# A hybrid layer on one core: the sum projection contracts over all 16 row tiles in PSUM, residual rows move into the last projection, ya is split one tile a product

## The chip, the core and the metric

The kernel runs on one core of a Trainium2 chip. A core has TensorE (PE, with its weight loads as PEld), VectorE (DVE), ScalarE (ACT), GpSimd (POOL) and SyncE (SP), each with its own queue of instructions that it takes in order, and DMA engines that SP, ACT and POOL hand transfers to. SBUF is the working memory on the chip, PSUM the eight banks of 128 x 512 fp32 that TensorE writes its products into. The metric is the time of one launch on the device in microseconds (us); the median of three runs before was 1457.02 us (1455.95 to 1457.52).

## The reference

One layer over 1024 positions and 1024 channels, fp32, tolerances of fp32. Cut to what matters here:

```python
h = layer_norm(x, ln_in_g, ln_in_b)
proj = h @ w_in                                  # u, b_gate, c_gate, z_a, z_s, xbc, dt, g_a, g_s
y_a = silu(z_a) * b_gate * conv3(c_gate * u)
y_a = y_a @ w_a_out                              # 1024 -> 1024, the first projection
y_s = ssd_scan(...) + d_skip * xs                # 2048 channels in 4 groups
y_s = gated_group_rmsnorm(y_s, z_s, norm_s_g)
y_s = y_s @ w_s_out                              # 2048 -> 1024, the sum projection
mixed = sigmoid(g_a) * y_a + sigmoid(g_s) * y_s
out = mixed @ w_o                                # 1024 -> 1024, the last projection
h = layer_norm(2 ** 0.25 * h + out, ln_g, ln_b)
```

## The kernel before

**Precision.** Every operand of a product is split into a high part (rounded to fp32r) and the rest: ACT copies the high part, and `sub_split` (L106) subtracts it from the full value. A product is three matmuls for each 128 rows of contraction: high by high, high by rest, rest by high (`mm3`, L799 to L802). One such split of 128 x 512 elements costs one ACT copy and one subtraction.

**The stages.** The input projection is 44 pairs of output tiles; each pair is seven products of 12 matmuls (a Strassen-like scheme, products 1, 2, 6, 5, 7, 4, 3 in this order, 3 behind the next pair's 1). While it runs, the scan of the state space is woven in, and its gated rows go to DRAM (`gat_d`, and per group the reciprocal root `rst_d`). Then come 16 items of the first projection `("a", j, kh)`, 24 matmuls each, 32 items of the sum projection `("s", g, j)`, 24 matmuls each, and the last projection, 8 rows of 128 positions.

**The order.** The loop over `items` writes out the instructions of item n, then what earlier items left in `sums` and `later` for n. Weights are fetched five items ahead, their high part is copied three items ahead and the rest two items ahead, so that in VectorE's queue the weight split of item n+2 stands before the sums of item n. `pin` keeps the written order on every engine from item 21 to the end of the loop; behind it, in the last projection, a scheduler sets the order.

**From the input projection to the first.** `start_post` loads the eight tiles of y_a (`ya`). In products 2, 6, 5 and 7 of pair 43 `halves` splits two of them each: four ACT copies (L771) and four subtractions on VectorE, beside that product's own weight split and adds (L954, L980, L982) that free its PSUM banks.

**The sum projection.** It goes group by group, g = 0 to 3, and in each over the eight output tiles j. Each item contracts over the four row tiles of its group into two fresh banks (`p_ws`); `item_s` adds that to `acc[j]` in SBUF: a copy on ACT for g = 0 (L891), an add on VectorE after (L893), for g = 2 also times sg plus yg (L895, L896), for g = 3 the last product with sg, the sum and the split of the result m (L899, L900, L902). The y tiles for group g are loaded and split on the way (`prep_y`, L781 to L789), one tile every other item: a broadcast of `rst_d` (rb), the tile gt, one three-operand product on VectorE (L789), two copies on ACT, two subtractions on VectorE.

**The residual rows** alpha * h are made on the way in groups 1 and 2 (`residual`): load x, normalise on ACT (L862), times ag and plus ab on POOL (L863, L864, 128 x 1024 each), store to `res_d`; the last projection loads them again.

**The last projection** (`project`, `norm_out`): per row of positions 48 matmuls into two banks, VectorE adds the residual and takes statistics (L1073, L1074), a chain of small operations gives mean and scale (L89 to L103), ACT normalises (L1090), POOL multiplies by lg and adds lb (L1091, L1092), SP stores. The last row does most of its columns on VectorE (L1086, L1087).

Of the kernel before, what the change touches and what calls it, by code (L numbers as in the profile page):

```python
# [45 lines left out]
def trunk_kernel(ctx: ExitStack, tc: tile.TileContext, x, w_in, w_dt, w_a, w_s, w_o, par, con,  # L46
# [97 lines left out]
    def otile(name):  # L144
        return ap.tile([P, L], F32, tag="O", name=name, bufs=4)
# [59 lines left out]
    items += [("s", g, j) for g in range(G) for j in range(KT)]  # L205
# [575 lines left out]
    def prep_y(g, k):  # L781

        rb = otile(f"rb{g}_{k}")
        SP.dma_start(rb, rst_d[g].squeeze(0).partition_broadcast(P))
        y = otile(f"gt{4 * g + k}")
        SP.dma_start(y, gat_d[g][:, k, :])

        def work():
            V.scalar_tensor_tensor(y, y, pc(C_NG + 4 * g + k), rb, ALU.mult, ALU.mult)  # L789
            halves(f"y{g}", k, y, True)  # L790
        later.setdefault(now[0] + (2 if items[now[0]][0] == "s" else 1), []).append(work)
# [41 lines left out]

    def split_wo(k, hf_i, u):
        r = rawt(f"raw_wo{k}_{hf_i}")
        SP.dma_start(r, w_o[k, :, hcols[hf_i]])
        WO[k, hf_i] = u

        def work():
            S.activation(u[:, 0, :], r, AF.Copy)  # L840
            sub_split(u[:, 1, :], r, u[:, 0, :], V)
        if hf_i:
            work()
        else:
            later.setdefault(now[0] + 1, []).append(work)

    norm_t = {}

    def residual(s):

        if s == 0:
            for i, (n, src) in enumerate((("ag", ln_in_g), ("ab", ln_in_b))):
                t = norm_t[n] = full_unit(POST[20 + i], n)
                SP.dma_start(t, src.partition_broadcast(P))
# [3 lines left out]
        def work():
            if s == 0:
                for t in norm_t.values():  # L860
                    S.activation(t, t, AF.Copy, scale=ALPHA)
            S.activation(r, r, AF.Identity, bias=nb_t[:, s:s + 1], scale=rs_t[:, s:s + 1])  # L862
            Gp.tensor_tensor(r, r, norm_t["ag"], ALU.mult)  # L863
            Gp.tensor_tensor(r, r, norm_t["ab"], ALU.add)  # L864
            Gp.dma_start(res_d[s], r)
        later.setdefault(now[0] + 1, []).append(work)

    def item_s(g, j, hi, lo):
        if g == 0:
            acc[j] = xtile(j, f"acc{j}") if j < 7 else cv("acc7")  # L870
        ps = [pbank(f"p_ws{g}_{j}_{i}") for i in range(2)]
# [6 lines left out]
        if g in (1, 2) and j % 2 == 0:
            residual(4 * (g - 1) + j // 2)
        if g == 1 and j == KT - 1:  # L880
            load_gy(0)
        if g == 2 and j < KT - 1:
            load_gy(j + 1)
        if g == 2 and j == KT - 1 or g == 3 and j < KT - 1:
            load_gy((j + 1) % KT, ("sg",))
        def evac():
            for hf_i in range(2):
                sl = hcols[hf_i]
                part = acc[j][:, sl]
                if g == 0:  # L890
                    S.activation(part, ps[hf_i], AF.Copy)  # L891
                elif g < 3:
                    V.tensor_tensor(part, ps[hf_i], part, ALU.add)  # L893
# [282 lines left out]
```

## Time and profile before

| | |
|---|---|
| runs before, median (lowest to highest) | 1457.02 us (1455.95 to 1457.52) |
| the profiled execution | 1455.73 us |
| its span on the core | 1454.0 us |
| mean granted TensorE clock | 0.989 |
| input projection up to the first matmul of the first projection | 1061.5 us |
| first projection | 1061.5 to 1151.1 us |
| sum projection | 1151.1 to 1356.7 us |
| last projection up to its last matmul, and the tail | 1356.7 to 1445.6 us, to 1454.0 |

A row of the timeline is: start in us, length in us, engine, line, operation, output<-inputs with their shape, and in brackets how long the engine sat idle before it and what released it. A length includes time in which the instruction had started and was held. Row groups end in "busy us, mean ns | idle before them, and what ended it". A stage table has PE, PEld, DVE, ACT and POOL busy (with instruction counts), the granted clock (1.00 is full), the share of the DMA engines and GB/s.

### The profile page before, as it was taken

Reading aid. Unit: us, or ns where it says so; the run is one execution under the profiler, and the core shown is the slowest. Engines: PE = TensorE matmul, PEld = TensorE weight load, DVE = VectorE, ACT = ScalarE, POOL = GpSimd, SP = SyncE. Lnnn points to the kernel's source line nnn. Section 1 sums busy time; section 2 is a strip of 40 time slices with the busy share of each in tenths; the row PEclk is TensorE's granted clock in tenths of the full one; section 3 lists DMA queues with packets and bytes.
Section 4 is the critical chain, followed back from the end, with each engine's and each line's share of the span. In section 5 each row is a group of like instructions: output and inputs, shape, how many; then the busy total and the mean of one; then the engine's idle time right before and its main releaser. Section 6 shows DMA issues by size and latency. Waiting matters only on the chain.

```text
span 1454.0 us, 18639 instructions
## 1 busy us (share of the span) xinstructions
PE 1396.3 (96%) x6522; PEld 1102.6 (76%) x6522; DVE 1022.1 (70%) x1495; ACT 716.0 (49%) x1243; POOL 481.0 (33%) x374
## 2 busy tenths in 40 slices
PE   6999999999999999999999999999899999959997
PEld 4677878787777878777878878787678888847786
DVE  7957878877788787787887585776534338778763
ACT  3664556555665655575645656555621233112321
POOL 4012334535244444335453344444000004331054
PEclk9999999999999999999999999999999999989999
DMA  6022354454454454454734545544547736567331
GB/s 231 16 109 80 112 144 128 137 159 133 142 130 136 138 155 123 137 131 135 172 118 134 161 125 150 151 124 138 218 162 242 232 118 218 213 212 288 131 127 62
DMA packets 171901, 217.02 MB, mean 149 GB/s; under 512 B 11520, under 2 KB 116896, under 8 KB 171808
## 3 DMA queue, kind: packets, MB, share of 16 engines
q1 hardware_dynamic: 162128, 181.80, 42.2%
q10 hardware_dynamic: 8272, 29.81, 5.2%
q0 software_dynamic: 1408, 4.23, 0.7%
q8 instruction: 51, 0.84, 0.2%
q14 instruction: 42, 0.34, 0.1%
HBM read 160.97 MB, written 54.82 MB: 148 GB/s over the span
## 4 chain that ended last, share of the span: by engine, by line
PE 80%; DVE 10%; DMA 5%; ACT 3%; issue 2%; ACTq 0%; SPq 0%; POOL 0%; POOLq 0%; DVEq 0%
PE p L945 10%; PE p L947 10%; PE p L946 10%; PE pU L947 8%; PE pU L945 8%; PE pU L946 8%; DMA yg<-yag_d 3%; PE ya L659 2%; PE p_ws L800 2%; PE p_ws L802 2%; PE p_ws L801 2%; PE p_wa L802 2%; PE p_wa L801 2%; PE p_wa L800 2%; PE st L664 2%
## 5 line engine op out<-in xcount | busy, mean ns | idle before, releaser
L106 DVE TENSOR_TENSOR wlop<-raw_a,whip 128x512 fp32r<-128x512 f32 x210 | 180.8, 861 | 171.4 <-ACT whip L276 66.7
L945 PE MATMUL p<-b,whip 128*128 128x512 f32 x352 | 144.0, 410 | 4.3 <-DVE ob L954 4.3
L945 PE MATMUL pU<-t,whip 128*128 128x512 f32 x352 | 144.7, 412 | 3.0 <-ACT oa L980 3.0
L276 ACT ACTIVATE whip<-raw_a 128x512 fp32r<-128x512 f32 x210 | 127.6, 622 | 36.9 <-issue 10.5
L945 PE MATMUL p<-t,whip 128*128 128x512 f32 x352 | 141.8, 403 | 1.5 <-DVE oa L954 1.5
L947 PE MATMUL p<-t,wlop 128*128 128x512 f32 x352 | 139.2, 395 | 1.5 <-DVE wlop L106 1.5
L946 PE MATMUL p<-b,whip 128*128 128x512 f32 x352 | 139.9, 398 | 0.0
L947 PE MATMUL p<-b,wlop 128*128 128x512 f32 x352 | 139.7, 397 | 0.0
L947 PE MATMUL pU<-t,wlop 128*128 128x512 f32 x352 | 139.0, 396 | 0.5 <-DVE wlop L106 0.4
L946 PE MATMUL p<-t,whip 128*128 128x512 f32 x352 | 138.9, 395 | 0.0
L946 PE MATMUL pU<-t,whip 128*128 128x512 f32 x352 | 138.9, 395 | 0.0
L644 POOL TENSOR_TENSOR xw<-xd,dte_t 128x256 f32<-128x256 f32 x56 | 47.0, 840 | 259.0 <-DVE xd L630 259.0
L802 PE MATMUL p_ws<-y,wlos 128*128 128x512 f32 x256 | 104.3, 408 | 12.4 <-DVE wlos L106 12.4
L801 PE MATMUL p_ws<-y,whis 128*128 128x512 f32 x256 | 103.9, 406 | 5.2 <-DVE y L106 5.2
L800 PE MATMUL p_ws<-y,whis 128*128 128x512 f32 x256 | 103.6, 405 | 0.0
L236 POOL TENSOR_TENSOR s<-raw_a,raw_a 128x512 f32<-128x512 f32 x42 | 69.5, 1654 | 85.1 <-DVE wlop L106 74.0
L250 POOL TENSOR_TENSOR raw_a<-raw_a,s 128x512 f32<-128x512 f32 x42 | 66.0, 1572 | 95.4 <-issue 87.4
L863 POOL TENSOR_TENSOR rs<-rs,ag 128x1024 f32<-128x1024 f32 x8 | 19.5, 2444 | 231.4 <-ACT rs L862 231.4
L945 PEld LDWEIGHTS p<-b,whip 128*128 128x128 f32 x352 | 66.8, 190 | 27.4 <-issue 8.8
L106 DVE TENSOR_TENSOR wlop<-s,whip 128x512 fp32r<-128x512 f32 x84 | 80.1, 966 | 9.4 <-PE p L947 6.3
L610 ACT ACTIVATE em<-em,cum_t 128x128 f32<-128x128 f32 x256 | 81.3, 390 | 7.3 <-ACT ob L554 4.4
L945 PEld LDWEIGHTS pU<-t,whip 128*128 128x128 f32 x352 | 66.1, 188 | 20.0 <-ACT oa L980 4.3
(223 smaller groups left out, 3353.7 us busy)
## 6 DMA issues: line engine op xcount, KB each, us to landing
raw_a<-in_w_in_dram SPq DMA_DIRECT2D x168, 256.0 KB
em<-cum_d SPq DMA_DIRECT2D x64, 256.0 KB
xg_d<-cv ACTq DMA_DIRECT2D x16, 512.0 KB
xT<-xg_d SPq DMA_DIRECT2D x32, 256.0 KB
z<-zs_d SPq DMA_DIRECT2D x32, 256.0 KB
gat_d<-y SPq DMA_DIRECT2D x32, 256.0 KB
rb<-rst_d SPq DMA_DIRECT2D x16, 512.0 KB
gt<-gat_d SPq DMA_DIRECT2D x16, 512.0 KB
```

What stands on the lines that cost most here:

```text
L106: return eng.tensor_tensor(lo, full, hi.bitcast(F32), ALU.subtract)
L236: Gp.tensor_tensor(s1, r["a21"], r["a22"], ALU.add)
L250: Gp.tensor_tensor(a12, a12, s1s[p]["s2"], ALU.subtract)
L276: S.activation(flat(hi), src, AF.Copy)
L610: S.activation(em[:, h, :], em[:, h, :], AF.Relu, bias=cum_t[:, 8 * g + 4 * i + h, c:c + 1], scale=-1.0)
L644: Gp.tensor_tensor(xw, XD[n, i], dte_t[:, hs, c].unsqueeze(2).to_broadcast([P, HG, HD]), ALU.mult)
L800: PE.matmul(ps, lhsT=hi[:, k, :], rhs=u[:, 0, :], start=start, stop=False)
L801: PE.matmul(ps, lhsT=hi[:, k, :], rhs=u[:, 1, :], start=False, stop=False)
L802: PE.matmul(ps, lhsT=lo[:, k, :], rhs=u[:, 0, :], start=False, stop=stop)
L945: PE.matmul(ps, lhsT=hi[:, k, :], rhs=u[:, 0, :], start=first, stop=False, skip_group_check=True)
L946: PE.matmul(ps, lhsT=hi[:, k, :], rhs=u[:, 1, :], start=False, stop=False, skip_group_check=True)
L947: PE.matmul(ps, lhsT=lo[:, k, :], rhs=u[:, 0, :], start=False, stop=(k == 3), skip_group_check=True)
```

## The change

- The sum projection keeps its partial sums in PSUM. The items of j = 0 to 2 run as a wave: groups 0 and 1 for the three, then groups 2 and 3 for the three, with six banks open; from j = 3 on the four groups of one j follow each other. `acc` is gone; one evacuation for each j, after its last group, multiplies by sg and adds yg in place.
- All 16 y tiles are split before their group is due: tiles 0 to 7 during the first projection, 8 to 15 at its end and in the first items of the sum projection, by a table of places. They stay in SBUF until the end of the sum projection. rb is loaded once a group.
- m is split later: first halves of tiles 0 to 6 and the first halves of w_o in the last three items, the rest behind the last item, ahead of the last projection's first row on VectorE's queue.
- `residual` writes no DRAM. Rows 0 to 2 are made ahead of the last projection, row s+3 behind `norm_out(s)`.
- The last projection's order is pinned too.
- ya: `turn_ya` splits one tile in each of the products 2, 6, 5, 7, 4 and 3 of pair 43 and two in the first item of the first projection; the second half's subtraction goes to POOL.

```diff
-    items += [("s", g, j) for g in range(G) for j in range(KT)]
+    WAVE = 3
+    s_order = [(g, j) for gs in ((0, 1), (2, 3)) for j in range(WAVE) for g in gs]
+    s_order += [(g, j) for j in range(WAVE, KT) for g in range(G)]
+    items += [("s", g, j) for g, j in s_order]
...
+    def turn_ya(k):
+        halves("a", k, ya_raw[k], (2 * k, 2 * k + 1), eng=Gp)
...
         def rests():
-            for u, part in zip(us, parts):
-                sub_split(u[:, 1, :], part, u[:, 0, :], V)
+            for u, part, e in zip(us, parts, (V, eng or V)):
+                sub_split(u[:, 1, :], part, u[:, 0, :], e)
...
+        if k == 0:
+            rb_t[g] = cv(f"rb{g}")
+            SP.dma_start(rb_t[g], rst_d[g].squeeze(0).partition_broadcast(P))
...
+    a0, s0 = item_at["a", 0, 0], item_at["s", 0, 0]
+    y_at = {}
+    for t, i in enumerate((1, 3, 5, 6, 8, 10, 11, 13, 14, 15, 16, 17, 18, 19, 19, 20)):
+        y_at.setdefault(a0 + i, []).append(t)
...
     def residual(s):
-        r = full_unit(POST[22 + s % 2], f"rs{s}")
-        SP.dma_start(r, x[s * P:(s + 1) * P, :])
...
-            Gp.dma_start(res_d[s], r)
+        r = res[s]
+        S.activation(r, r, AF.Identity, bias=nb_t[:, s:s + 1], scale=rs_t[:, s:s + 1])
+        Gp.tensor_tensor(r, r, norm_t["ag"], ALU.mult)
+        Gp.tensor_tensor(r, r, norm_t["ab"], ALU.add)
...
-                mm3(ps[hf_i], hi, lo, k, Y[f"y{g}", k, hf_i], k == 0, k == 3)
+                mm3(ps[hf_i], hi, lo, k, Y["y", 4 * g + k, hf_i], g == 0 and k == 0, g == G - 1 and k == 3)
...
-                if g == 0:
-                    S.activation(part, ps[hf_i], AF.Copy)
-                elif g < 3:
-                    V.tensor_tensor(part, ps[hf_i], part, ALU.add)
...
+                V.tensor_tensor(M[j][:, sl], ps[hf_i], M[j][:, sl], ALU.mult)
+                V.tensor_tensor(M[j][:, sl], M[j][:, sl], gy[j][:, sl], ALU.add)
+                if j == KT - 1:
+                    split_m(j, hf_i, post_unit(31 if hf_i == 0 else 15, f"m{j}_{hf_i}"))
...
+    def split_m(j, hf_i, u):
+        part = M[j][:, hcols[hf_i]]
+        M[j, hf_i] = u
+        S.activation(u[:, 0, :], part, AF.Copy)
+        sub_split(u[:, 1, :], part, u[:, 0, :], V)
...
+    for n in norm_t.values():
+        S.activation(n, n, AF.Copy, scale=ALPHA)
+    residual(0)
+    for k in range(4, KT):
+        split_wo(k, 1, post_unit(4 + k, f"wo{k}_1"))
+    residual(1)
+    load_res(2)
+    for k, i in enumerate((12, 13, 14, 33, 34, 32)):
+        split_m(k, 1, post_unit(i, f"m{k}_1"))
+    split_m(6, 1, ap.tile([P, 2, HALF], F32R, tag="cv", name="m6_1", bufs=2))
+    load_norm("lg", ("c", 0), ln_g)
+    load_norm("lb", ("o", 2), ln_b)
+    residual(2)
...
-            if i == NP - 1 and j in (2, 6, 5, 7):
+            if i == NP - 1 and j in (2, 6, 5, 7, 4, 3):
...
-                for k in range(2):
-                    kk = 2 * (2, 6, 5, 7).index(j) + k
-                    halves("a", kk, ya_raw[kk])
+                turn_ya((2, 6, 5, 7, 4, 3).index(j))
...
         norm_out(s, 3 if s == NCH - 1 else 2)
+        if s + 3 < NCH:
+            residual(s + 3)
+        pin(True)
```

**VectorE, from pair 43 into the first projection.** Names: a_k0 and a_k1 are the halves of tile k of ya, wlop43_j the rest of the weights of product j of pair 43, wloa the same for the first projection, ob43 an output tile of pair 43 whose adds free the bank that the pair's last product needs. Before:

```order
L106 TENSOR_TENSOR a_41_9534<-ya4_9439,a_41_9534 128x512
L106 TENSOR_TENSOR a_50_9539<-ya5_9441,a_50_9539 128x512
L106 TENSOR_TENSOR a_51_9540<-ya5_9441,a_51_9540 128x512
L106 TENSOR_TENSOR wlop43_3_9549<-raw43_a12_9242,whip43_3_9516 128x512
L106 TENSOR_TENSOR a_60_9565<-ya6_9443,a_60_9565 128x512
L106 TENSOR_TENSOR a_61_9566<-ya6_9443,a_61_9566 128x512
L106 TENSOR_TENSOR a_70_9571<-ya7_9445,a_70_9571 128x512
L106 TENSOR_TENSOR a_71_9572<-ya7_9445,a_71_9572 128x512
L106 TENSOR_TENSOR wloa0_0_9581<-raw_a0_0_9480,whia0_0_9547 128x512
L954 TENSOR_TENSOR ob43_9551<-p4_43_9520,ob43_9551 128x512
```

Now, from the same place (its lines are those of the changed file):

```order
L106 TENSOR_TENSOR a_10_9488<-ya1_9425,a_10_9488 128x512
L106 TENSOR_TENSOR wlop43_4_9498<-raw43_a22_9238,whip43_4_9468 128x512
L106 TENSOR_TENSOR a_20_9513<-ya2_9427,a_20_9513 128x512
L106 TENSOR_TENSOR wlop43_3_9523<-raw43_a12_9234,whip43_3_9496 128x512
L106 TENSOR_TENSOR a_30_9539<-ya3_9429,a_30_9539 128x512
L106 TENSOR_TENSOR wloa0_0_9549<-raw_a0_0_9466,whia0_0_9521 128x512
L988 TENSOR_TENSOR ob43_9525<-p4_43_9500,ob43_9525 128x512
```

Ahead of that add of ob43 stand four subtractions of ya (a_00, a_10, a_20, a_30) where sixteen stood; the second halves are on POOL's queue.

**VectorE, behind the last evacuation of the sum projection.** wo_k_1 is the second half of tile k of w_o, m_k_1 the second half of tile k of the mixed rows, res0 the first residual row. Now:

```order
L106 TENSOR_TENSOR wo4_1_11429<-raw_wo4_1_11396,wo4_1_11429 128x512
L106 TENSOR_TENSOR wo5_1_11432<-raw_wo5_1_11398,wo5_1_11432 128x512
L106 TENSOR_TENSOR wo6_1_11435<-raw_wo6_1_11400,wo6_1_11435 128x512
L106 TENSOR_TENSOR wo7_1_11438<-raw_wo7_1_11402,wo7_1_11438 128x512
L106 TENSOR_TENSOR m0_1_11446<-sg0_10476,m0_1_11446 128x512
L106 TENSOR_TENSOR m1_1_11449<-sg1_10551,m1_1_11449 128x512
...
L106 TENSOR_TENSOR m6_1_11464<-sg6_11109,m6_1_11464 128x512
L1119 TENSOR_TENSOR res0_11408<-p_wo0_0_11476,res0_11408 128x512
```

All splits of m's second halves stand before the first row's evacuation; before, the splits of m came with the evacuations of group 3.

**POOL, in the last projection.** res_s is residual row s; ag, ab belong to the residual, lg, lb to the output. Before:

```order
L1091 TENSOR_TENSOR res0_11691<-res0_11691,lg_11551 128x1024
L1092 TENSOR_TENSOR res0_11691<-res0_11691,lb_11553 128x1024
L1091 TENSOR_TENSOR res1_11693<-res1_11693,lg_11551 128x1024
L1092 TENSOR_TENSOR res1_11693<-res1_11693,lb_11553 128x1024
L1091 TENSOR_TENSOR res2_11695<-res2_11695,lg_11551 128x1024
L1092 TENSOR_TENSOR res2_11695<-res2_11695,lb_11553 128x1024
```

Now:

```order
L1137 TENSOR_TENSOR res0_11408<-res0_11408,lg_11467 128x1024
L1138 TENSOR_TENSOR res0_11408<-res0_11408,lb_11469 128x1024
L904 TENSOR_TENSOR res3_11584<-res3_11584,ag_11404 128x1024
L905 TENSOR_TENSOR res3_11584<-res3_11584,ab_11406 128x1024
L1137 TENSOR_TENSOR res1_11410<-res1_11410,lg_11467 128x1024
L1138 TENSOR_TENSOR res1_11410<-res1_11410,lb_11469 128x1024
```

Between two normalised rows POOL now makes one residual row, three rows ahead; ahead of these rows it makes residual rows 0 to 2.

More of the change, by code (lines that the diff above doesn't have):

```diff
@@ L142, in full_unit, with otile @@
         return hp.tile([P, L], F32, tag=f"q{i}", name=name)
-    def otile(name):
-        return ap.tile([P, L], F32, tag="O", name=name, bufs=4)
+    n_o = [0]
+    def otile(name, i=None):
+        if i is None:
+            i = n_o[0] % 4
+            n_o[0] += 1
+        return ap.tile([P, L], F32, tag=f"O{i}", name=name)
     def cv(name):
@@ L779, in halves, with place, prep_y @@
             rests()
[L781 to L785, printed above, removed]
+    YP = list(range(16, 32)) + list(range(16))
+    GT = [("x", 4), ("x", 5), ("x", 6), ("o", 2), ("o", 3)]
+    rb_t = {}
+    def place(where, name):
+        kind, i = where
+        return xtile(i, name) if kind == "x" else otile(name, i) if kind == "o" else cv(name)
+    def prep_y(t):
+        g, k = divmod(t, 4)
+        if k == 0:
+            rb_t[g] = cv(f"rb{g}")
+            SP.dma_start(rb_t[g], rst_d[g].squeeze(0).partition_broadcast(P))
+        rb = rb_t[g]
+        y = place(GT[t % 5], f"gt{t}")
         SP.dma_start(y, gat_d[g][:, k, :])
         def work():
-            V.scalar_tensor_tensor(y, y, pc(C_NG + 4 * g + k), rb, ALU.mult, ALU.mult)
-            halves(f"y{g}", k, y, True)
-        later.setdefault(now[0] + (2 if items[now[0]][0] == "s" else 1), []).append(work)
+            V.scalar_tensor_tensor(y, y, pc(C_NG + t), rb, ALU.mult, ALU.mult)
+            halves("y", t, y, YP[2 * t:2 * t + 2], True)
+        later.setdefault(now[0] + 1, []).append(work)
     n_bank = [0]
@@ L847, in trunk_kernel, with load_gy @@
-    norm_t = {}
-    def residual(s):
[L851 to L854, printed above, removed]
-        r = full_unit(POST[22 + s % 2], f"rs{s}")
-        SP.dma_start(r, x[s * P:(s + 1) * P, :])
[L858 to L864, printed above, removed]
-            Gp.dma_start(res_d[s], r)
-        later.setdefault(now[0] + 1, []).append(work)
+    def load_gy(j):
+        M[j] = place(SG[j], f"sg{j}")
+        SP.dma_start(M[j], sgs_d[j])
+        gy[j] = otile(f"yg{j}", j % 2 if j < KT - 1 else 0)
+        SP.dma_start(gy[j], yag_d[j])
@@ L868, in item_s @@
     def item_s(g, j, hi, lo):
         if g == 0:
-            acc[j] = xtile(j, f"acc{j}") if j < 7 else cv("acc7")
-        ps = [pbank(f"p_ws{g}_{j}_{i}") for i in range(2)]
+            sy[j] = [pbank(f"p_ws{j}_{i}") for i in range(2)]
+        ps = sy[j]
         for hf_i in range(2):
             for k in range(4):
-                mm3(ps[hf_i], hi, lo, k, Y[f"y{g}", k, hf_i], k == 0, k == 3)
-        if g < 3 and j in (1, 3, 5, 7)[:4 if g < 2 else 2]:
-            y_next = 4 * g + 6 + j // 2
-            prep_y(y_next // 4, y_next % 4)
@@ L878, in item_s @@
[L878 to L885, printed above, removed]
+                mm3(ps[hf_i], hi, lo, k, Y["y", 4 * g + k, hf_i], g == 0 and k == 0, g == G - 1 and k == 3)
         def evac():
@@ L1027, in trunk_kernel @@
             item_a(i, j, hi, lo)
+            if i == 0 and j == 0:
+                turn_ya(6)
+                turn_ya(7)
         else:
             item_s(i, j, hi, lo)
+        for t in y_at.get(n, ()):
+            prep_y(t)
+        if n in gy_at:
+            load_gy(gy_at[n])
         if n == START - 1:
@@ L1093, in norm_out @@
         SP.dma_start(out[s * P:(s + 1) * P, sl], r[:, sl])
-    for s in range(3):
-        load_res(s)
     for s in range(NCH):
```

114 lines of the change are left out of this document (59 added, 55 removed).

## The prediction

> **What bounds the kernel now.** First the page's busy shares and the chain that ended last.
>
> ```profile
> PE 1396.3 (96%) x6522; PEld 1102.6 (76%) x6522; DVE 1022.1 (70%) x1495; ACT 716.0 (49%) x1243; POOL 481.0 (33%) x374
> PE 80%; DVE 10%; DMA 5%; ACT 3%; issue 2%; ACTq 0%; SPq 0%; POOL 0%; POOLq 0%; DVEq 0%
> ```
>
> TensorE carries four fifths of the chain, so the question is where it is not at its pace. Next, busy time by stage: the first projection (p_wa), the sum projection (p_ws) and the last one (p_wo), from first matmul to first matmul. The columns are PE, PEld, DVE, ACT and POOL busy with instruction counts, then granted clock, DMA share and GB/s.
>
> ```profile
> 1061.50:1151.10 89.60, 89.60 (x385) 71.81 (x385) 34.87 (x49) 19.05 (x30) 0.00 (x0) 1.00 0.64 214
> 1151.10:1356.70 205.60, 187.94 (x769) 148.20 (x769) 137.29 (x166) 60.17 (x98) 46.07 (x24) 0.96 0.60 206
> 1356.70:1445.60 88.90, 88.61 (x409) 73.03 (x407) 51.00 (x100) 17.84 (x26) 33.60 (x14) 1.00 0.28 107
> ```
>
> The first projection issues 384 matmuls in 89.6 us without a gap: 0.2333 us each, at clock 1.00. The sum projection has twice as many, 768, of the same shape, and would take 179.2 us. It takes 205.6: **26.4 us lost**, at clock 0.96. What PE waited for there, with total, times and longest, and its rows behind two kinds of waits:
>
> ```profile
> PE p_ws L802 <- DVE wlos L106: 12.4, 6, 3.6
> PE p_ws L801 <- DVE y L106: 5.2, 1, 5.2
> 1278.55 0.51 PE L802 MATMUL p_ws<-y,wlos 128*128 128x512 f32 x1 [3.58 <-DVE wlos L106]
> ...
> 1279.68 0.63 PE L802 MATMUL p_ws<-y,wlos 128*128 128x512 f32 x1
> 1280.11 0.63 PE L800 MATMUL p_ws<-y,whis 128*128 128x512 f32 x1
> ...
> 1288.61 0.50 PE L802 MATMUL p_ws<-y,wlos 128*128 128x512 f32 x1 [2.63 <-DVE wlos L106]
> ...
> 1344.23 0.50 PE L802 MATMUL p_ws<-y,wlos 128*128 128x512 f32 x1 [1.39 <-DVE wlos L106]
> ```
>
> The waits are 17.6 us, all for VectorE. The other 8.8 are their sequel: behind a long wait matmuls stand 0.43 us apart (1279.68 to 1280.11) instead of 0.23. So VectorE bounds this stage. Why it is late is in the rows of POOL and DVE side by side:
>
> ```profile
> 1196.81 1.28 DVE L106 TENSOR_TENSOR y<-gt,y 128x512 fp32r<-128x512 f32 x2
> 1209.18 2.40 POOL L863 TENSOR_TENSOR rs<-rs,ag 128x1024 f32<-128x1024 f32 x1 [167.70 <-ACT rs L862]
> 1211.65 2.72 POOL L864 TENSOR_TENSOR rs<-rs,ab 128x1024 f32<-128x1024 f32 x1
> 1209.21 5.72 DVE L106 TENSOR_TENSOR y<-gt,y 128x512 fp32r<-128x512 f32 x2
> L893 DVE TENSOR_TENSOR acc<-p_ws,acc 128x512 f32<-128x512 f32 x32 | 21.1, 679 | 0.0
> ```
>
> Two subtractions of y take 1.28 us alone, and 5.72 beside two POOL operations: each ends only behind the POOL operation that it met. I call this **the lock**; one VectorE operation with two SBUF inputs gets through per POOL operation. Operations that read PSUM are not held: L893 means 679 ns over the same stretch.
>
> **Part 1, the sum projection.** The change removes its 16 ACT and 32 DVE partial sums, moves all of y's splits ahead of their use, and moves the residual's POOL work out of the stage. Per four items of 5.6 us VectorE keeps four weight splits and one evacuation of four operations: 8 x 0.68 = 5.5 us of 22.4, with POOL idle. Each y tile costs about 2.6 us of DVE (1.28 for L789, 1.28 for its two subtractions), beside gates (L821) and weight splits (the last row):
>
> ```profile
> L789 DVE SCALAR_TENSOR_TENSOR gt<-gt,par_t,rb 128x1024 f32<-128x1024 f32 x16 | 20.4, 1278 | 8.8 <-DMA gt<-gat_d 8.8
> L821 DVE TENSOR_TENSOR sga<-p_wa,sga 128x512 f32<-128x512 f32 x16 | 10.2, 681 | 0.0
> L106 DVE TENSOR_TENSOR wlos<-raw_s,whis 128x512 fp32r<-128x512 f32 x32 | 22.0, 687 | 49.9 <-issue 28.5 <-PE p_ws L802 9.8 <-PE p_wa L802 6.9
> ```
>
> Sixteen tiles over the 22 items from a1 on are 42 us, beside 10.2 of gates and 15 of weight splits: 67 of 123 us. The order puts the last y work one item ahead of (3,0), which needs it, and a weight split two items ahead of its matmuls, so an 11 us delay is hidden. SP's queue also carries less: rb is loaded 4 times instead of 16. With 16 gt, 8 sga and 8 yag of 0.5 MB and 22 weights of 0.26 that is about 25 MB in 123 us, 200 GB/s, where the first projection moved 214 without holding PE. Here sga of row j+2 waits on SP for the store of row j, and gt and raw stand behind it; the store goes out 2 us after its gate, so SP is some 11 us ahead of need. I take **-26.4**, from -26.4 to -18 if half of the waits find another cause.
>
> **Part 2, ya.** From pair 43 into the first projection, PE stops four times:
>
> ```profile
> PE p L945 <- DVE oa L954: 1.5, 1, 1.5
> PE pU L945 <- ACT oa L980: 1.6, 1, 1.6
> PE p L947 <- DVE wlop L106: 1.5, 1, 1.5
> 1057.13 0.77 PE L945 MATMUL p<-b,whip 128*128 128x512 f32 x1 [4.11 <-DVE ob L954]
> 1061.55 0.39 PE L800 MATMUL p_wa<-a,whia 128*128 128x512 f32 x1
> 1049.22 2.17 ACT L771 ACTIVATE a<-ya 128x512 fp32r<-128x512 f32 x4
> 1053.29 2.49 DVE L106 TENSOR_TENSOR a<-ya,a 128x512 fp32r<-128x512 f32 x4
> 1056.30 0.68 DVE L954 TENSOR_TENSOR ob<-p,ob 128x512 f32<-128x512 f32 x1
> 1040.18 1.29 POOL L250 TENSOR_TENSOR raw_a<-raw_a,s 128x512 f32<-128x512 f32 x1
> ```
>
> A product is 12 matmuls, 2.8 us; two tiles in it cost ACT 2.17 and DVE 2.49 us beside their other work. With one tile ACT pays 1.1, DVE 0.6 and POOL 1.3 (L250 has its shape). The first stop is older and stays. The second loses the 1.1 us of ACT. The fourth, which starts the slow clock, hangs on the first add to ob43: ACT's copy of pU at about 1049.7 (after the copies of three tiles instead of six), then DVE's row order a_30, wloa0_0, ob43. Without the lock that add ends at 1052.1 and the first projection starts at 1054.9: 6.6 earlier. But POOL's subtractions stand just there, each 1.3 us, and a_10, wlop43_4, a_20, wlop43_3, a_30, wloa0_0 meet five of them. With the lock I get ob43 at 1055.0, PE waiting 4 us as now, the same 4.4 us of slow product behind it (1057.13 to 1061.55), and the start at 1059.5. I take **-2.0**, nearer to the end with the lock because its row is of this kernel; bounds -6.6 and 0. The Trainium skill (Perfetto Trace Analysis, Optimizing Scalar/DVE Operations) warns that moving operations between GpSimd and VectorE may not help, since they share an SBUF read port; by that this term is 0 and the sum 2 us higher.
>
> **Part 3, into the last projection.** Let E be the end of the sum projection. Evacuation of j = 7 for the first half starts at E-2.8 and is four operations of 0.7: m7_0 is there at E, and PE uses it 21 matmuls behind E. Hidden; if VectorE were behind by 5 us it would show.
>
> ```profile
> L840 ACT ACTIVATE wo<-raw_wo 128x512 fp32r<-128x512 f32 x16 | 9.2, 619 | 2.8 <-PE p_ws L802 2.1 <-DMA raw_wo<-in_w_o_dram 0.7
> L861 ACT ACTIVATE ag<-ag 128x1024 f32<-128x1024 f32 x1 | 1.0, 1042 | 0.0
> ```
>
> ACT then copies m7_1 (E+2) and four wo halves (9.2 us for 16 while busy, so to E+4.3), scales ag and ab and makes res0, three operations of that size (to E+7.5), and only then copies wo4_1 to wo7_1 (to E+9.8). POOL starts res0 at E+7.6 and holds the port for four operations to E+18. DVE's subtractions of wo4_1 to wo7_1 get through one per POOL operation: E+10.6, 13.3, 15.8, 18.5. PE's third group (row 0, second half) starts at E+11 and wants them at 13.9, 14.6, 15.3, 16.0 or, once late, just behind: it stops for 0.5 and 2.1 us. I take **+2.6**; 0 if POOL starts late, 5 if each slot takes 3.3 us. Row 1288.61 shows that 2.63 us can bring the slow clock, row 1344.23 that 1.39 doesn't; two stops add nothing or up to 1.8, within that bound. (The Trainium skill, TensorE: Matmul & The Clock Gate, What's actually happening, puts the drop at an idle window of about 3.4 us; by that it adds nothing, though row 1288.61 came earlier.)
>
> **Part 4, the rows.** A row of the last projection takes PE 10.97 us (1423.38 to 1434.36); POOL has two operations of 2.4 in it, and gets two more:
>
> ```profile
> 1423.38 0.69 DVE L1073 TENSOR_TENSOR res<-p_wo,res 128x512 f32<-128x512 f32 x1 [4.01 <-PE p_wo L1072]
> 1434.36 0.69 DVE L1073 TENSOR_TENSOR res<-p_wo,res 128x512 f32<-128x512 f32 x1 [4.01 <-PE p_wo L1072]
> 1427.62 2.41 POOL L1091 TENSOR_TENSOR res<-res,lg 128x1024 f32<-128x1024 f32 x1 [6.09 <-ACT res L1090]
> 1430.11 2.40 POOL L1092 TENSOR_TENSOR res<-res,lb 128x1024 f32<-128x1024 f32 x1
> 1388.65 2.39 POOL L1091 TENSOR_TENSOR res<-res,lg 128x1024 f32<-128x1024 f32 x1 [66.69 <-ACT res L1090]
> 1389.25 1.80 DVE L93 SCALAR_TENSOR_TENSOR lob<-rs,loa 128x1 f32<-128x1 f32 x1
> 1445.59 0.42 DVE L1073 TENSOR_TENSOR res<-p_wo,res 128x256 f32<-128x256 f32 x1 [1.99 <-PE p_wo L1072]
> 1448.56 1.08 DVE L1087 SCALAR_TENSOR_TENSOR res<-res,rs,lb 128x832 f32<-128x832 f32 x1
> ```
>
> That is 2.4 + 2.7 + 2.4 + 2.4 and gaps: 10.1 us, just under PE's 10.97. VectorE's small operations L93, L97, L103 meet the lock too (1389.25 ends with POOL's operation), up to 3 x 2.45 us a row with some 3.3 of others: 10.7. All three engines are within 10%. On SP each residual's load stands behind the store of an earlier row: res6 goes out at E+56, ACT wants it at E+60; 4 us for 0.5 MB, at the 200 GB/s above 2.6 us and its latency. VectorE's splits of wo and m end at E+23, rows 0 and 1 are evacuated by E+28, the first normalised row reaches POOL at E+31, and 12 pairs of 5 us from there end at E+93 for row 6, while PE ends at E+91.5. The last row's L1086 and L93 then wait behind POOL: L1087 ends 5.4 us after PE instead of 4.1 (1445.55 to 1449.64). I take **+1.3**, from 0 (POOL starts earlier) to 5 (one pair late). The stores and loads of res_d go; their traffic held nobody.
>
> **Sum.** -26.4 - 2.0 + 2.6 + 1.3 = -24.5. The profiled execution took 1455.73 us (span 1454.0), 1.3 under the median of 1457.02, so the time is 1431.
>
> **Rivals.** (a) The lock bites less: POOL meets few of the splits, ya gains all, parts 3 and 4 cost nothing. 1455.7 - 26.4 - 6.6 = 1423. For it: the lock's rows are of 128 x 1024 operations, POOL's on ya have half that; against: row 1209.21, where not one subtraction slipped through. Chance 0.15. (b) A new wait takes the old one's place, y late for (2,0) and (3,0), or POOL one pair late in the rows: 1431 + 8 = 1439. For it: three engines within 10% of a row; against: the first projection's clean 89.60. Chance 0.15. (c) POOL returns nothing for ya: 1433, chance 0.12. (d) Slower: in the last projection each row becomes a ring, POOL waiting for DVE's row and DVE for POOL's lock. A ring would be 10.1 + 3.3 + two ACT operations of 1.04 = 15.5 us; 4.5 over PE's pace in 8 rows is 36 us, so 1431 + 36 = 1467. It decides from 3.1 us a row over PE's pace. Against: the order puts the next residual between two normalised rows, which needs neither. Chance 0.04. (e) The change doesn't do what it says, the accumulation stops for banks (six of eight are held by a wave) and the time stays: 1457, chance 0.02; against: in the order j = 0 is evacuated eight items before j = 4 takes its banks.
>
> **Numbers.** Forecast 0.52. The range takes (a), (c) and the bounds of parts 2 to 4: 1422 to 1441. Faster by over 0.2% (3 us, about what a measurement here can tell) 0.94, same 0.02, slower 0.04.
>
> **What would show it.** Right: p_ws first to last near 179 us at clock 1.00 with no wait for wlos or y; the first projection 2 us earlier; two short stops of p_wo for wo; POOL busy over 85% from E+31. Wrong: PE waiting at (2,0) for y, or DVE waiting on gt; row intervals over 11.5 us.

## The result, and the profile after

The changed kernel takes **1434.28 us** in the median (1433.79 to 1434.54, 4 runs), beside 1457.07 us (4 runs) of the kernel before: a ratio of 0.9843, 95% interval 0.9828 to 0.9857. The forecast was 1431. Its profiled execution took 1434.14 us (span 1432.2) against 1455.73 (span 1454.0).

First the busy line of the page, then the stage table of the first projection, the sum projection and the last one, from first matmul to first matmul, the last stage up to VectorE's addition of the last product (columns as before the change).

```profile
PE 1391.3 (97%) x6522; PEld 1100.9 (77%) x6522; DVE 975.1 (68%) x1423; ACT 708.8 (49%) x1227; POOL 484.7 (34%) x374
```

```profile
1060.72:1150.50 89.78, 89.78 (x385) 71.97 (x384) 42.57 (x58) 24.35 (x40) 3.02 (x2) 1.00 0.70 237
1150.50:1329.40 178.90, 178.90 (x769) 143.69 (x768) 68.86 (x101) 35.48 (x59) 0.00 (x0) 1.00 0.39 131
1329.40:1422.39 92.99, 90.51 (x409) 74.16 (x407) 64.18 (x93) 31.96 (x41) 72.78 (x30) 0.98 0.27 95
```

The sum projection now has no gap: its span and PE's busy time are the same 178.90 us, at clock 1.00, and VectorE's work in it has halved (137.29 to 68.86). The last projection went the other way: 88.9 to 92.99, at clock 0.98, with POOL busy for 72.78 instead of 33.60. Side by side with the terms of the prediction:

| where | predicted | measured |
|---|---|---|
| start of the first projection | -2.0 | 1061.55 to 1060.72: -0.8 |
| first projection | 0 | 89.6 to 89.8: +0.2 |
| sum projection | -26.4 | 205.6 to 178.9: -26.7 |
| last projection, to its last addition | +2.6 | 88.9 to 93.0: +4.1 |
| from there to the end | +1.3 | 8.4 to 9.8: +1.4 |
| sum | -24.5 | -21.8 |

Three places hold what is left. The rows of the timeline of the changed kernel between pair 43 and the first projection:

```profile
1041.46 0.47 PE L979 MATMUL p<-t,whip 128*128 128x512 f32 x1 [1.71 <-DVE oa L988]
...
1044.09 1.80 DVE L106 TENSOR_TENSOR wlop<-raw_a,whip 128x512 fp32r<-128x512 f32 x1
...
1050.65 0.63 ACT L279 ACTIVATE whia<-raw_a 128x512 fp32r<-128x512 f32 x1 [1.61 <-DMA raw_a<-in_w_a_dram]
...
1052.88 1.28 POOL L106 TENSOR_TENSOR a<-ya,a 128x512 fp32r<-128x512 f32 x1 [2.32 <-DMA raw_a<-in_w_a_dram]
1052.93 1.78 DVE L106 TENSOR_TENSOR wloa<-raw_a,whia 128x512 fp32r<-128x512 f32 x1
1054.64 0.68 DVE L988 TENSOR_TENSOR ob<-p,ob 128x512 f32<-128x512 f32 x1
1055.46 0.76 PE L979 MATMUL p<-b,whip 128*128 128x512 f32 x1 [3.41 <-ACT a L781]
...
1060.72 0.61 PE L822 MATMUL p_wa<-a,whia 128*128 128x512 f32 x1
```

The lock shows on 512 columns too: a subtraction of 0.68 us lasts 1.78 when it meets a POOL subtraction of 1.28, and L988, which reads PSUM, stays at 0.68. It ends at 1055.3 (forecast 1055.0), and PE's last product starts there; the row names ACT, whose copy ended about then too. The product then takes 5.26 us, all of it at the slow clock (forecast 4.4). Not foreseen is ACT's 1.61 us at 1050.65, for a weight load. In the last projection:

```profile
1337.42 10.87 DVE L106 TENSOR_TENSOR wo<-raw_wo,wo 128x512 fp32r<-128x512 f32 x4 [2.53 <-ACT wo L881]
1339.43 2.74 POOL L905 TENSOR_TENSOR res<-res,ab 128x1024 f32<-128x1024 f32 x1
1342.13 2.83 POOL L904 TENSOR_TENSOR res<-res,ag 128x1024 f32<-128x1024 f32 x1
...
1345.57 0.50 PE L1117 MATMUL p_wo<-wo,m 128*128 128x512 f32 x1 [0.64 <-DVE wo L106]
...
1348.34 0.80 PE L1117 MATMUL p_wo<-wo,m 128*128 128x512 f32 x1 [1.80 <-DVE wo L106]
1348.93 0.63 PE L1118 MATMUL p_wo<-wo,m 128*128 128x512 f32 x1
```

Four subtractions take 10.87 us, one for each POOL operation; PE stops twice, 0.64 and 1.80 us (forecast 0.5 and 2.1), and behind the second its matmuls are slow (0.63 where others have 0.39). And the tail:

```profile
1418.15 2.42 POOL L1138 TENSOR_TENSOR res<-res,lb 128x1024 f32<-128x1024 f32 x1
...
1424.11 0.22 DVE L93 SCALAR_TENSOR_TENSOR lob<-rs,loa 128x1 f32<-128x1 f32 x1
...
1424.63 1.08 DVE L1132 SCALAR_TENSOR_TENSOR res<-res,mv,lg 128x832 f32<-128x832 f32 x1
1425.74 1.08 DVE L1133 SCALAR_TENSOR_TENSOR res<-res,rs,lb 128x832 f32<-128x832 f32 x1
1426.91 0.37 ACTq L1134 DMA_DIRECT2D out_dram<-res  x1
1427.33 0.55 ACT L1136 ACTIVATE res<-res,nb,rs 128x192 f32<-128x192 f32 x1 [3.46 <-DVE res L1133]
```

POOL is done at 1420.6, so L93 takes 0.22 and nothing here is locked, against the forecast; but L1132 stands behind the whole chain, and ACT's last operation behind a store that waits for L1133.

### The profile page after: what moved, and what is told of

Its sections match the earlier page's. It is cut to its first block, busy times and chain, and to the rows that moved or that the text cites. A ratio compares the mean times of both kernels' runs of the same rounds, so it can differ in the third digit from the quotient of the medians.

```text
span 1432.2 us, 18457 instructions
## 1 busy us (share of the span) xinstructions
PE 1391.3 (97%) x6522; PEld 1100.9 (77%) x6522; DVE 975.1 (68%) x1423; ACT 708.8 (49%) x1227; POOL 484.7 (34%) x374
## 5 line engine op out<-in xcount | busy, mean ns | idle before, releaser
L904 POOL TENSOR_TENSOR res<-res,ag 128x1024 f32<-128x1024 f32 x8 | 19.6, 2455 | 276.4 <-ACT res L903 271.6
L823 PE MATMUL p_ws<-y,whis 128*128 128x512 f32 x256 | 100.9, 394 | 0.0
L822 PE MATMUL p_ws<-y,whis 128*128 128x512 f32 x256 | 100.8, 394 | 0.0
L824 PE MATMUL p_ws<-y,wlos 128*128 128x512 f32 x256 | 100.7, 393 | 0.0
L106 DVE TENSOR_TENSOR wlos<-raw_s,whis 128x512 fp32r<-128x512 f32 x32 | 22.1, 692 | 113.0 <-PE p_ws L824 89.3
```

Of the source, the lines that this page charges most:

```text
L106: return eng.tensor_tensor(lo, full, hi.bitcast(F32), ALU.subtract)
L822: PE.matmul(ps, lhsT=hi[:, k, :], rhs=u[:, 0, :], start=start, stop=False)
L823: PE.matmul(ps, lhsT=hi[:, k, :], rhs=u[:, 1, :], start=False, stop=False)
L824: PE.matmul(ps, lhsT=lo[:, k, :], rhs=u[:, 0, :], start=False, stop=stop)
```

## The experiments

For each kernel the table has the median and, from its profile, four lengths: from the matmul behind pair 43's first stop (1041.46 in the changed kernel) to the first matmul of the first projection ("ya"); the sum projection; the last projection to the start of its last addition; from there to the end of the span ("tail"). Counting from that stop leaves out that executions reach it at different times (1040.59 to 1042.28 us), which no edit here touches. Ratios are against runs of the kernel before on the same chip, whose medians were 1457.1 to 1458.7; so medians a microsecond apart are not told apart here, and the lengths carry the argument.

| kernel | median us | ratio (95%) | ya | sum | last | tail |
|---|---|---|---|---|---|---|
| before | 1457.07 | 1 | 20.88 | 205.6 | 88.9 | 8.4 |
| changed | 1434.28 | 0.9828 to 0.9857 | 19.26 | 178.9 | 93.0 | 9.8 |
| before_nopool | 1439.15 | 0.9856 to 0.9883 | 20.88 | 188.2 | 88.8 | 7.9 |
| pool_in_sum | 1432.62 | 0.9819 to 0.9846 | 17.95 | 178.9 | 93.1 | 9.8 |
| undo_ya | 1434.99 | 0.9833 to 0.9860 | 20.87 | 178.9 | 91.6 | 9.8 |
| ya_dve | 1429.46 | 0.9793 to 0.9820 | 17.18 | 178.9 | 91.6 | 9.8 |
| ya_order | 1434.11 | 0.9821 to 0.9848 | 17.30 | 178.9 | 93.2 | 9.9 |
| ya_order2 | 1427.60 | 0.9774 to 0.9800 | 13.34 | 178.9 | 91.6 | 9.8 |
| ya_order2_dve | 1427.91 | 0.9775 to 0.9802 | 12.71 | 178.9 | 93.2 | 9.8 |
| wo_first | 1429.86 | 0.9794 to 0.9821 | 18.41 | 178.9 | 88.6 | 9.8 |
| tail_act | 1434.60 | 0.9829 to 0.9856 | 19.14 | 178.9 | 93.0 | 9.7 |
| unpin_last | 1430.99 | 0.9807 to 0.9834 | 18.13 | 178.9 | 93.0 | 8.4 |
| best1 | 1429.16 | 0.9791 to 0.9818 | 17.31 | 178.9 | 88.6 | 9.3 |
| best2 | 1423.02 | 0.9745 to 0.9772 | 13.34 | 178.9 | 88.6 | 8.8 |

Five kernels have the changed kernel's own order between pair 43 and the first projection (changed, pool_in_sum, wo_first, tail_act, unpin_last): their "ya" is 17.95 to 19.26, mean 18.6. The spread has one source: in all five the last product of pair 43 starts 13.86 to 14.00 us behind the first stop, and then takes 4.06 to 5.26 us, by how many of its matmuls run at the slow clock. So that start is the steadier measure: with two tiles of ya a product it is 16.46 us (before) and 16.45 (undo_ya).

### What held the sum projection

Was it the lock alone? The kernel before, without the residual's two POOL operations:

```diff
-            Gp.tensor_tensor(r, r, norm_t["ag"], ALU.mult)
-            Gp.tensor_tensor(r, r, norm_t["ab"], ALU.add)
             Gp.dma_start(res_d[s], r)
```

> The kernel before with the two GpSimd operations of each residual row left out of the sum projection (its output then lacks their gain and offset); partial sums, y's splits and all loads stay. Theory A (GpSimd's operations hold VectorE, and that alone costs the stage its 26.4 us): waits for wlos and y nearly go, the stage takes 179 to 184 us instead of 205.6, the time is 1430 to 1436. Theory B (partial sums and y's splits put too much on VectorE in any case): waits remain, the stage takes 195 us or more, 1446 or more. In between, both hold a share, and the number gives it.

The stage takes 188.2 us, in between the two theories: the lock's share is 17.4 of the 26.7. Its stage row, and rows of its timeline that show what is left:

```profile
1152.20:1340.40 188.20, 181.47 (x770) 145.10 (x769) 111.54 (x166) 60.43 (x98) 4.28 (x8) 0.99 0.65 225
```

```profile
1265.12 0.69 DVE L893 TENSOR_TENSOR acc<-acc,sg 128x512 f32<-128x512 f32 x1 [3.36 <-DMA sg<-sgs_d]
...
1281.90 0.69 DVE L893 TENSOR_TENSOR acc<-acc,sg 128x512 f32<-128x512 f32 x1 [2.65 <-DMA sg<-sgs_d]
...
1294.93 0.80 PE L801 MATMUL p_ws<-y,whis 128*128 128x512 f32 x1 [4.00 <-DVE y L106]
```

VectorE stands on the partial sums of group 2, waiting for the load of sg, while the splits of y and of weights for group 3 queue behind; PE then stops for 4.00 us and runs slowly after. Two waits for weight splits add 2.7 us. The kernel before has the same waits of VectorE:

```profile
1272.65 0.69 DVE L895 TENSOR_TENSOR acc<-acc,sg 128x512 f32<-128x512 f32 x1 [4.18 <-DMA sg<-sgs_d]
```

That is a second cause, by these rows; it was not taken away by itself, so its 9 us are argued and not shown. The other corner is the changed kernel with as many POOL operations as the stage had before:

```diff
+        m = now[0] - s0
+        if m >= 8 and m % 2 == 0 and m < 24:
...
+            for _ in range(2):
+                Gp.tensor_tensor(spare[0], u, u, ALU.mult)
```

> The changed kernel with sixteen GpSimd multiplications of 128 x 1024 put into the sum projection, two in every second item from its ninth on, where the kernel before had its residual; their product goes to a spare tile that nothing reads. With the operations left out of the kernel before, its stage fell from 205.6 to 188.2 us, so 17.4 of the 26.4 hung on GpSimd and 9 on the rest. Theory A (the two add up: with the partial sums gone VectorE has room, and a held split is two items ahead of its use): the stage stays under 185 us and the time under 1441. Theory B (the lock alone costs its 17 us whatever else VectorE has to do): 178.9 + 17 = 196 us, 1451.

Its stage, and two groups of rows within the stage:

```profile
1149.60:1328.50 178.90, 178.90 (x770) 143.74 (x769) 79.29 (x101) 35.47 (x59) 33.59 (x16) 1.00 0.39 131
```

```profile
L916 POOL TENSOR_TENSOR spare<-y 128x1024 bf16<-128x1024 f32 x16 | 33.6, 2100 | 122.2 <-DVE y L106 121.0
L106 DVE TENSOR_TENSOR wlos<-raw_s,whis 128x512 fp32r<-128x512 f32 x30 | 26.4, 880 | 96.4 <-PE p_ws L824 73.1 <-issue 23.3
```

Theory A: the stage is as long as without them, to a tenth of a microsecond. POOL still holds VectorE (a weight split means 880 ns instead of 692), but VectorE is busy for 79 us of 179, and a split is due two items later. The dose is smaller than before, though: these operations last 2.10 us, the residual's 2.4 to 2.7, and they lengthen VectorE's busy time by 10.4 us (68.86 to 79.29), where the residual's lengthened it by 25.8 (111.54 to 137.29, with the same 166 operations). So 10.4 us of holding cost nothing here, and 25.8 cost 17.4 us there: whether the holding costs time hangs on the slack of the engine that is held. That the full 25.8 would be free here too was not shown.

### What the split of ya brings

The changed kernel, with ya split two tiles a product on VectorE, as before:

```diff
-        halves("a", k, ya_raw[k], (2 * k, 2 * k + 1), eng=Gp)
+        halves("a", k, ya_raw[k], (2 * k, 2 * k + 1))
...
-            if i == 0 and j == 0:
-                turn_ya(6)
-                turn_ya(7)
...
-            if i == NP - 1 and j in (2, 6, 5, 7, 4, 3):
+            if i == NP - 1 and j in (2, 6, 5, 7):
...
-                turn_ya((2, 6, 5, 7, 4, 3).index(j))
+                for k in range(2):
+                    turn_ya(2 * (2, 6, 5, 7).index(j) + k)
```

> The changed kernel with ya split as before: two tiles a product in the first four products of the last pair, all subtractions on VectorE, GpSimd without any. My theory (the split one tile a product brought some 1.6 us, and GpSimd's subtractions gave back most of what it could have brought): the wait of pU for ACT's oa is 1.6 us again instead of 0.54, no subtraction lasts over 0.7 us, the wait ahead of the last product is 4.1 us again, and the first projection starts 1.2 to 2.0 us later than in the changed kernel: 1435.5 to 1436.3. Rival (the split moved nothing, the difference of 0.85 us was the two executions' own): the same start within 0.4 us, 1434.3.

```profile
1058.72 0.47 PE L979 MATMUL p<-b,whip 128*128 128x512 f32 x1 [4.12 <-DVE ob L988]
```

"ya" is 20.87, the length of before (20.88): the split is worth 1.6 us against the changed kernel's profile, 2.3 against the mean of the five, and 2.5 at the start of the last product. The median rose by only 0.7; in the profile 1.4 us of the loss come back in the last projection, 91.6 instead of 93.0, at the same two stops:

```profile
1347.78 0.50 PE L1115 MATMUL p_wo<-wo,m 128*128 128x512 f32 x1 [0.64 <-DVE wo L106]
...
1350.55 0.50 PE L1115 MATMUL p_wo<-wo,m 128*128 128x512 f32 x1 [1.80 <-DVE wo L106]
1350.89 0.40 PE L1116 MATMUL p_wo<-wo,m 128*128 128x512 f32 x1
```

Here no slow clock follows. Does GpSimd's share help? One tile a product, all on VectorE:

```diff
-        halves("a", k, ya_raw[k], (2 * k, 2 * k + 1), eng=Gp)
+        halves("a", k, ya_raw[k], (2 * k, 2 * k + 1))
```

> The changed kernel in its own order, one tile of ya a product, but with all subtractions of ya on VectorE and none on GpSimd. Theory A (the gain of the ya split is the smaller dose a product, and GpSimd's share gives nothing because each of its subtractions holds one of VectorE's for 1.1 us): the first projection starts 0.3 to 1.5 us earlier than in the changed kernel, measured from the first stop of the last pair (20.95 us there, from 1041.46 minus its wait to 1060.7), and the time is 1433 to 1434.5. Theory B (GpSimd's share is what brings the gain): without it VectorE has 0.68 us more a tile, the first projection starts 1 us or more later, 1435.3 or more.

17.18 us: shorter than in any of the five with GpSimd, by 0.8 to 2.1; the last product starts 12.78 us behind the stop, 1.1 to 1.2 us earlier than in the five. Its rows:

```profile
1051.94 0.68 DVE L106 TENSOR_TENSOR wloa<-raw_a,whia 128x512 fp32r<-128x512 f32 x1
1052.54 0.68 DVE L988 TENSOR_TENSOR ob<-p,ob 128x512 f32<-128x512 f32 x1
...
1053.37 0.77 PE L979 MATMUL p<-b,whip 128*128 128x512 f32 x1 [2.71 <-DVE ob L988]
```

With nobody to meet, wloa takes 0.68 us. So the smaller dose brought the gain (20.88 to 17.18) and GpSimd gave part of it back. The median, 4.8 us lower and below either expectation, overstates this: in the profiles 2.1 us are this term, 0.9 an earlier arrival at pair 43's stop, and 1.4 a last projection without the slow clock.

The rest of the wait is order. ACT's copy and VectorE's first addition of ob43 were put ahead:

```diff
-        else:
+        elif items[n] != ("p", NP - 1, 7):
...
+            if items[n] == ("p", NP - 1, 7):
+                for f in sums.pop(n + 1):
+                    f()
+                prep_hi(n + LA)
+                prep_lo(n + LA - 1)
```

> The changed kernel, with two moves at the last pair's sixth product: ACT's copy of pU into ob ahead of the copy of whia0_0 (which waited 1.61 us for its load), and VectorE's first addition to ob43 right behind it, ahead of wlop43_3, a_30 and wloa0_0; all subtractions stay where they are, GpSimd's too. Theory A (the wait of 3.41 us ahead of the last product and the slow product behind it come from the order of this addition behind held splits, not from too much work): the addition ends at about 1051.7 to 1052.3, the last product starts at 1052.1 to 1052.6 instead of 1055.46, without the slow clock, and the first projection at 1055 to 1056.5 instead of 1060.7: 1430 to 1431.5. Theory B (ACT and VectorE are full here, so wlop43_3 or the a tiles come late instead): new waits for wlop or a of 3 us and more, the first projection not before 1059, 1433 or more.

Both theories hold a part. The product starts at once, without its 3.41 us; the wait moves on to the next PSUM addition in VectorE's queue, which frees the first bank of the first projection:

```profile
1052.61 0.40 PE L979 MATMUL p<-b,whip 128*128 128x512 f32 x1
...
1052.99 1.82 POOL L106 TENSOR_TENSOR a<-ya,a 128x512 fp32r<-128x512 f32 x1 [1.70 <-ACT a L781]
1053.56 1.79 DVE L106 TENSOR_TENSOR wloa<-raw_a,whia 128x512 fp32r<-128x512 f32 x1
1055.28 1.77 DVE L106 TENSOR_TENSOR a<-ya,a 128x512 fp32r<-128x512 f32 x1
1056.97 1.76 DVE L106 TENSOR_TENSOR wloa<-raw_a,whia 128x512 fp32r<-128x512 f32 x1
1058.65 0.68 DVE L988 TENSOR_TENSOR ob<-p,ob 128x512 f32<-128x512 f32 x1
...
1059.48 0.77 PE L822 MATMUL p_wa<-a,whia 128*128 128x512 f32 x1 [3.79 <-DVE ob L988]
```

The slow clock moves with it into the first projection (91.2 us instead of 89.8), and the time stays, as theory B had it, though for a bank and not for the operands. So the second addition was put ahead too (the same lines, for product 4 as well):

> As the run with ob43's first addition ahead, and ob43's second addition (of the product before the last, whose bank the first projection needs) also ahead: on VectorE it stands behind a_30 and before wloa0_0, instead of behind a_40 and wloa0_1. Both additions read PSUM. There the first projection waited 3.79 us for this second addition, which ended at 1059.3 behind three subtractions of 1.77 to 1.79 us beside GpSimd's. Theory A (each wait here is the place of one PSUM addition behind held splits): the second addition ends at 1053.6 to 1054.5, the first projection starts at 1055.3 to 1056.3, and at most 1.5 us of new waits (a_40 to a_70) follow within it: 1429.5 to 1431. Theory B (VectorE with the lock is full, so the lateness goes on to wloa or a): new waits of 2.5 us and more at wloa0_0, wloa0_1 or a_40 to a_70 with the slow clock, and the first projection ends where it did, near 1150: 1433.5 to 1434.5.

```profile
1053.65 0.68 DVE L988 TENSOR_TENSOR ob<-p,ob 128x512 f32<-128x512 f32 x1
...
1055.62 0.39 PE L822 MATMUL p_wa<-a,whia 128*128 128x512 f32 x1
```

"ya" is 13.34, 5.9 us shorter than in the changed kernel's profile and 5.2 than the mean of the five, without a wait ahead of the first projection or in it: the operands had slack, the bank additions had none. The median, 1427.60, is below both expectations; 1.4 us of that are a last projection without the slow clock. The same with all subtractions on VectorE:

> The same with both additions ahead, and all subtractions of ya on VectorE, none on GpSimd. If GpSimd's subtractions hold VectorE by 1.1 us each and VectorE's own take 0.68 us, this kernel's VectorE has its work done earlier than with GpSimd: no subtraction over 0.75 us from 1043 to 1062, first projection at the same start or up to 1 us earlier, and its waits inside are shorter; time equal to that run or up to 2 us less. If there is no lock for operations of 512 columns, VectorE has eight subtractions (5.5 us) more to do and the first projection is 2 us or more later.

12.71 instead of 13.34: with the additions in place the lock costs 0.6 us, and the two medians (1427.91, 1427.60) can't be told apart.

### The stops in the last projection

```diff
+    for k in range(4, KT):
+        split_wo(k, 1, post_unit(4 + k, f"wo{k}_1"))
     for n in norm_t.values():
         S.activation(n, n, AF.Copy, scale=ALPHA)
     residual(0)
-    for k in range(4, KT):
-        split_wo(k, 1, post_unit(4 + k, f"wo{k}_1"))
```

> The changed kernel with the splits of wo4_1 to wo7_1 ahead of the scaling of ag and ab and of the first residual row. My theory (the two stops of p_wo, 0.64 and 1.80 us, and the slow clock behind them come from wo splits held behind GpSimd's residual): the four subtractions last 0.69 us each, both stops and the slow clock go, the last matmul comes 89.0 us behind the end of the sum projection instead of 92.95, and the time falls by 3.5 to 4.0: 1430.3 to 1430.8. Rival 1 (the rows are paced by GpSimd, which now starts 2 us later): stops go, but rows come at GpSimd's pace and the end moves by 1 us or less, 1433.3 or more. Rival 2 (the stops were not due to the lock): they stay, 1434.3.

```profile
1331.35 4.90 DVE L106 TENSOR_TENSOR wo<-raw_wo,wo 128x512 fp32r<-128x512 f32 x8
```

Eight subtractions now take 4.90 us where four took 10.87. Both stops are gone and the stage takes 88.6 us: -4.4 in the stage and in the median. POOL starts 9.6 us into the stage instead of 7.5 and still does not pace the rows.

### The tail

```diff
-            S.dma_start(out[s * P:(s + 1) * P, :cut], r[:, :cut])
         S.activation(r[:, sl], r[:, sl], AF.Identity, bias=nb, scale=rs)
+        if last_row:
+            S.dma_start(out[s * P:(s + 1) * P, :cut], r[:, :cut])
```

> The changed kernel with the store of the last row's first 832 columns put behind ACT's normalisation of the other 192 on ACT's queue, instead of ahead of it. Theory A (the tail is longer than before because this store waits on ACT's queue for VectorE's second operation and holds the normalisation of the 192 columns behind it): ACT starts that operation 3.1 us behind the last matmul's addition instead of 4.94, the end comes 8.0 to 8.5 us behind the last matmul instead of 9.8, so -1.3 to -1.8: 1432.5 to 1433.0. Theory B, that of the prediction (VectorE's row is held by GpSimd's last rows): the end does not move, 1434.3.

ACT's operation started 2.42 us behind the last addition instead of 4.94 (3.1 expected), and the end moved by 0.1 (9.7): the store of 832 columns, which waits for L1133, came no earlier, and POOL's last operation now meets L1133 and takes 1.25 us instead of 0.59. Theory A fell in this form. Then the whole last row was left to the scheduler:

```diff
-        pin(True)
+        pin(s < NCH - 1)
```

> The changed kernel, with the last row's instructions not held to the order of the code: as in the kernel before, VectorE's L1132 then stands between L90 and L91 (in the shadow of ACT's root) and ACT's 192 columns ahead of the store of the 832. With that store alone moved, the end stayed 9.7 us behind the last matmul. Theory A (the tail is 1.3 us longer because of the order, in which VectorE's second operation, and so the store of 832 columns, comes some 0.4 us later and the two stores follow each other closely or late): the end comes 8.3 to 8.7 us behind the last matmul's end, as before the change: -1.1 to -1.5, about 1433. Theory B (something else makes the end later, such as GpSimd's rows): 9.6 to 9.9, 1434.3.

```profile
1422.13 1.08 DVE L1132 SCALAR_TENSOR_TENSOR res<-res,mv,lg 128x832 f32<-128x832 f32 x1
1423.12 0.16 DVE L91 RECIPROCAL rs<-lob 128x1 f32<-128x1 f32 x1
...
1424.02 0.55 ACT L1136 ACTIVATE res<-res,nb,rs 128x192 f32<-128x192 f32 x1 [1.66 <-DVE nb L103]
...
1424.95 0.37 ACTq L1134 DMA_DIRECT2D out_dram<-res  x1
```

8.4 us, the tail of before: L1132 runs while ACT takes the root, and both stores go out earlier. The tail's 1.4 us are the pinned order of the last row, on two engines at once; VectorE's order was not freed by itself. The median fell by 3.3, in part because "ya" in this profile is also 1.1 us shorter, by the slow clock.

### Together

wo_first, ya_order and unpin_last in one kernel:

> The changed kernel with three edits at once: the splits of wo4_1 to wo7_1 ahead of the first residual, ob43's copy and addition ahead, and the last row's order left free. If the terms add (4.4 measured for the first; 3 to 4.5 expected of the second; 1.3 of the third): 1424.0 to 1425.5. If GpSimd then paces the rows, which start earlier with it, or the new order gives nothing: 1428 to 1430.

1429.16, within the second range: the new order gives nothing ("ya" 17.31, with the wait moved to the next bank). The tail is 9.3 us, 0.9 over unpin_last; 0.3 of that is an operation of VectorE held by POOL (L1137, 1.41 us), the rest is open. With ya_order2 in its place:

> Both additions ahead, the splits of wo4_1 to wo7_1 ahead of the first residual, and the last row's order free. With these last two and the first addition alone it took 1429.16. If the second addition brings 4 us: 1424.5 to 1426. If the lateness goes on to the first projection's operands: 1428.5 to 1429.5.

1423.02 us, 11 below the changed kernel and somewhat below the 1424.5 expected; "ya" and last are those of the single edits (13.34, 88.6). The tail is 8.8 instead of 8.4, for a reason that the prediction had put into the changed kernel:

```profile
1413.51 1.42 DVE L1137 SCALAR_TENSOR_TENSOR res<-res,mv,lg 128x832 f32<-128x832 f32 x1
```

Here TensorE ends early enough for POOL's row 6, done at 1414.05, to be in the way, and the operation lasts 1.42 instead of 1.08.

## Why the prediction was right, and where it was not

The forecast of 1431 was 3.3 us below the measured 1434.28, and the range held it.

- **Part 1**, -26.4 against -26.7: the size was right, the cause half right. The step that failed is the one that reads all 17.6 us of waits as the lock; without POOL's work 9 us of loss stayed, 6.7 of them waits of PE, with VectorE waiting for sg among the partial sums of group 2. The prediction allowed for that in its bound of -18. The change removes both causes, so the sum did not show the error.
- **Part 2**, -2.0: the start came 0.8 us earlier, the distance from pair 43's first stop fell by 1.6 in this profile and by 2.3 over five. The working for ob43 was nearly right: its addition ends 13.86 us behind that stop, where the forecast's 1055.0 puts it at 14.33. The "start at 1059.5" came out at 1060.72 because this execution reached pair 43 0.8 us later than the one of before, and because the slow product took 5.26 us, where the prediction took the 4.4 of before. ACT's wait of 1.61 us is no reason for the miss, as the addition was early in spite of it. The bound "6.6 without the lock" was too large for this order: ya_dve, without POOL's share, has no lock and gains 3.7; the rest needs the additions moved. Rival (c) said that POOL returns nothing and priced the whole term at 0. It was right on POOL's share, which costs 1.1 to 1.2 us, and wrong on the term: the gain is the dose. The warning of the Trainium skill (Perfetto Trace Analysis, Optimizing Scalar/DVE Operations) about moving work between these two engines held.
- **Part 3**, +2.6 against +4.1: the mechanism came as told, stop by stop, and without the slow clock the stage takes 91.6 (+2.7). The slow clock behind the second stop, costed at nothing with a bound of 1.8, came and cost 1.4.
- **Part 4**, +1.3 against +1.4: the size was right by luck. The step "L1086 and L93 then wait behind POOL" failed: POOL was done at 1420.6, L93 took 0.22, and VectorE's last operation ended 4.5 us after PE, not 5.4. The prediction's own figures say as much: 12 pairs of 5 us from E+31 end at E+91 to E+92, not at E+93, and POOL ended at E+91.2, while PE ended at E+92.9. What cost the time was the pinned order of the last row, with its stores (unpin_last). POOL's pace was right: it works without a gap from E+31 to 1413.9, and no row of PE waits.
- **Rivals (b), (d) and (e)** did not come: the sum projection has no wait for y or for a bank, rows are 11.1 us apart. (a) fell with the stops of part 3.

## What to carry to other kernels

When two engines share a path, ask first how much slack the held one has: sixteen POOL operations cost 17.4 us beside a queue whose splits were late already, and sixteen somewhat shorter ones nothing beside a queue with its work two items ahead. In an in-order queue put the operations that free an accumulator bank ahead of those that prepare operands; here that was worth 5 us, and moving only the first of two such operations moved the wait and nothing else. When an order is pinned, read the last row of it against what the scheduler had done.

## What the runs showed of the hardware

The same pair of stops, 0.64 and 1.80 us with three matmuls between them, was followed by slow matmuls (0.63 us) in six of nine profiles and by none in three (undo_ya, ya_dve, ya_order2); the price is 1.4 to 1.6 us of the stage (93.0 to 93.2 against 91.6). So in these profiles the slow clock behind these stops comes in some executions and not in others. The Trainium skill (TensorE: Matmul & The Clock Gate, What's actually happening) describes a free-running window of about 3.4 us, which fits that; that it takes an idle window of that length does not fit, as neither stop reaches it.

The lock goes both ways: POOL's subtraction of 512 columns took 1.28 us at 1052.88 in the changed kernel, and 1.82 at 1052.99 in ya_order. What decides it was not tried.
